# Both halves of a LayerNorm-closed output projection by Strassen-Winograd products, with some sums made by adding DMAs

## The chip, the core and the metric

The kernel runs on one NeuronCore of one Trainium2 chip. The metric is the time of one execution on the device in microseconds, median of three runs. Beside it stands one profiled execution, whose trace gives a start and a duration for every instruction. The engines are PE (matrix products; PEld is its weight load), DVE (vector), ACT (scalar), POOL (GpSimd) and SP, which only issues DMAs.

## The reference, cut to what matters

One step of a hybrid encoder layer for a prompt of 256 tokens and a running stream of 32, 288 rows together, width 1024. A single input projection feeds an mLSTM branch and a sparse attention branch. Both are gated and mixed, and the mix goes through the output projection, a residual and a LayerNorm:

```python
mixed = jax.nn.sigmoid(ga) * (branch_a @ w_out_a) + jax.nn.sigmoid(gb) * (branch_b @ w_out_b)
return layer_norm(DN_ALPHA * x + mixed @ w_o, ln_g, ln_b)
```

Everything is float32. The outputs besides the rows `y` are keys, values, indexer keys and the mLSTM states `C`, `n`, `m`. The change touches `mixed @ w_o` for the 256 prompt rows, the LayerNorm behind it, and the order in which the last outputs are stored.

## The kernel before, in words

**Two halves for every number.** PE multiplies in a rounded format (`F32R`). Each operand is split into a high half (rounded by an ACT copy) and a low half (raw minus high, a DVE subtraction, line 194 or 176). A product is three matmuls: high times high, high times low, low times high (lines 1062 to 1064 for projections, `group`, line 1073, for the output projection).

**Tiles and their order.** `tile_order` (line 60) lists the weight tiles of 128 columns by 1024 rows; each is one stage of 24 matmuls on PE, 3.2 us. The last sixteen are `ga`, `wa` in turn for j = 0 to 7. `WO` is the position of the first of the eight tiles of `w_o`. The main loop (line 1298) issues in each stage t: loads (`load_plan`, line 89), the low half of tile t + 2, the evacuation of tile t - 1, the high half of tile t + 3, then the 24 matmuls, with `side()` in their middle, which runs the jobs that `at(slot, ...)` put there. The order in which instructions are written is the order of every queue; nothing reorders them. Pairs of split tiles (`wh`, `wl`) rotate through four buffers each, raw tiles through eight `wst` buffers.

**Evacuating the mixed rows.** `wa` tile j (line 1005) gives rows 128 j to 128 j + 127 of the transposed mix `mB`, and their halves `mxh`, `mxl`; POOL copies the 32 sample columns to `mxs` (line 1014).

**The output projection** (`finish`, line 1159). The prompt rows form two blocks (rows 1 and 2), the contraction of 1024 is cut in two halves, and the output columns in two. The first half of the contraction (512) is done by Winograd's form of Strassen's scheme with seven block products: sums of token blocks s1 to s4 (`token_sums`, line 1017) and of weight blocks t1 to t4 (`weight_sum`, line 1034, four DVE subtractions). `seventh` (line 1079) is one such product: two contraction blocks of 128, three matmuls of 512 columns each. The second half is done plainly: `plain` (line 1085), four quarters of twelve matmuls. The partial results gather in PSUM banks `y11`, `y12`, `y21`, `y22`; `begun` and `added` (DVE, lines 1163 and 1167) put them onto the residual `z`, reading one bank twice where two outputs share a sum. `sample_rows` (line 1091) does the 32 sample rows in 64 small matmuls from raw tiles.

**The end.** `recorded` and `centred` take the statistics and centre rows, `scaled` multiplies by the reciprocal deviation (made by POOL's power, line 1156) and adds the bias. The first 128 rows are scaled and stored (line 1247) before the second 128 rows are begun. `state_prompt(h)` (line 776) makes the state of head h: twelve matmuls, two ACT copies, and a store, by SP for heads 0 and 1, by ACT for 2 and 3. In program order: first rows' store; second rows' centring; states 0 to 2; second rows' scaling and two stores by halves; state 3.

Of the kernel before, what the change touches and what calls it, by code (L numbers as in the profile page):

```python
# [14 lines left out]
OP = mybir.AluOpType  # L15
# [16 lines left out]
SEVEN = ("b11", "b21", "t2", "t1", "t3")  # L32
# [53 lines left out]
EARLY = WO - 20  # L86


def load_plan():
    slots, homes = defaultdict(list), {}  # L90
    for t in range(FIRST, EARLY + 9):
        slots[max(t - 9, FIRST)].append(t)
        homes[t] = (t - FIRST) % 8
    for i in range(4):
        slots[EARLY + i].append(WO + i)
        homes[WO + i] = (EARLY + 9 + i - FIRST) % 8
    rest = [*range(EARLY + 9, WO), *range(WO + 4, NT)]
    for i, t in enumerate(rest):
        slots[EARLY + 4 + i].append(t)
        homes[t] = (EARLY + 13 + i % 4 - FIRST) % 8  # L100
    return slots, homes
# [10 lines left out]
def body(ctx, tc, a, o):  # L112
# [37 lines left out]
    def load_tile(t):  # L150
        if t >= NT or t in loaded:
            return
        loaded.add(t)
        stage[t] = sb(f"wst{t}", [128, KT * 128], tag=f"wst{HOMES[t]}")
        sp.dma_start(stage[t], a["w"][:, t - FIRST])
# [5 lines left out]
    def raw_unit(u):  # L161
        if u[0] == "t":
            return lazy["sums"][u]
        if u[0] == "b":
            return stage[POS["wo", ("b11", "b12", "b21", "b22").index(u)]]
        return stage[POS["wo", int(u[1])]]
# [7 lines left out]
    def unit_lo(u):  # L174
        wh, wl = split[u]
        dve.tensor_tensor(wl, raw_unit(u), wh.bitcast(F32), OP.subtract)

# [30 lines left out]
    zeros = sb("zeros", [128, 128], BF)  # L208
# [95 lines left out]
    wn = sb("wn", [128, 8])  # L304
    wp0 = sb("wp0", [128, 4])
    ws = sb("ws", [128, 2])
# [628 lines left out]
    def evac(t, p):  # L935
# [69 lines left out]
        elif n == "wa":  # L1005
            if j == 0:
                lazy["mxh"] = sb("mxh", [128, 8, T], F32R, tag="a4")
                lazy["mxl"] = sb("mxl", [128, 8, T], F32R, tag="a2")
                lazy["mxs"] = sb("mxs", [128, 8, TS])
# [5 lines left out]
            halves("mxh", "mxl", j, mx)  # L1015

    def token_sums():
        m = lazy["mB"]
        a11, a12 = m[:, 0:2, 0:128], m[:, 2:4, 0:128]
        a21, a22 = m[:, 0:2, 128:256], m[:, 2:4, 128:256]  # L1020
        s1, s2, s3, s4 = (lazy["sraw"][:, i].rearrange("p (k t) -> p k t", k=2) for i in range(4))
# [5 lines left out]
    def token_halves():  # L1027
        both = sb("sums", [128, 2, 4, 256], F32R, tag="kaT")
        act.copy(both[:, 0], lazy["sraw"])
        dve.tensor_tensor(both[:, 1], lazy["sraw"], both[:, 0].bitcast(F32), OP.subtract)  # L1030
        for i in range(4):
            lazy["s", i + 1] = tuple(both[:, e, i].rearrange("p (k t) -> p k t", k=2) for e in range(2))

    def weight_sum(name):
        if "sums" not in lazy:
            t = sb("t123", [128, 3, KT * 128], tag="a5")
            lazy["sums"] = {"t1": t[:, 0], "t2": t[:, 1], "t3": t[:, 2], "t4": sb("t4", [128, KT * 128], tag="wmat")}
        first, second = {"t1": ("b12", "b11"), "t2": ("b22", "t1"), "t3": ("b22", "b12"), "t4": ("b21", "t2")}[name]
        dve.tensor_tensor(lazy["sums"][name], raw_unit(first), raw_unit(second), OP.subtract)

    at(WO - 6, token_sums)
    at(WO - 4, token_halves)
    for i, n in enumerate(("t1", "t2", "t3", "t4")):
        at(EARLY + 5 + 2 * i, weight_sum, n)
# [22 lines left out]
    def standing(n):  # L1067
        if n[0] == "s":
            return lazy["s", int(n[1])]
        k, r = 2 * (n[2] == "2"), 128 * (n[1] == "2")  # L1070
        return tuple(lazy[m][:, k:k + 2, r:r + 128] for m in ("mxh", "mxl"))
# [7 lines left out]
    def seventh(p, x, u, first=False):  # L1079
        x = standing(x)  # L1080
# [4 lines left out]
    def plain(p, rows, column, first=False):  # L1085
        r = slice(128 * rows, 128 * rows + 128)
        for k in range(4, KT):
            group(p, (lazy["mxh"][:, k, r], lazy["mxl"][:, k, r]), split[f"w{k}"],
                  slice(512 * column, 512 * column + 512), first and k == 4, k == KT - 1)

    def sample_rows(p):
        for k in range(KT):
            for q in range(4):
                if k < 4:
                    w, c = stage[POS["wo", 2 * (k // 2) + q // 2]], 512 * (k % 2) + 256 * (q % 2)
                else:
                    w, c = stage[POS["wo", k]], 256 * q
# [33 lines left out]
    def load_tail():  # L1131
        lazy["xn"] = sb("xn", [128, 2, D], tag="vaT")
        sq = sb("sq", [128, 8, 256], tag="stC")
        lazy["zs"], lazy["gs"], lazy["bs"], lazy["xs"] = (sq[:, i] for i in range(4))
        lazy["sraw"] = sq[:, 4:8]
        lazy["bst"] = sb("bst", [128, 2, 2, 6], tag="sg", bufs=3)
        lazy["bss"] = sb("bss", [128, 4, 6])
        sp.dma_start(lazy["xn"], a["x_nat"][0:TP].rearrange("(b p) c -> p b c", p=128))
        sp.dma_start(lazy["xs"], ap_of(a["x_nat"], TP * D, [[256, 4], [D, TS], [1, 256]]))

    def load_affine():
        gb = sb("rest", [128, 2, D], tag="xhl")
        lazy["g"], lazy["b"] = gb[:, 0], gb[:, 1]
        sp.dma_start(gb, ap_of(a["ln_gb"], 0, [[0, 128], [D, 2], [1, D]]))
# [6 lines left out]
    def statistics(b, r, records):  # L1151
        mv = sb(f"mv{b}", [128, 2])
        nr = sb(f"nr{b}", [128, 2])
# [5 lines left out]
    def finish():  # L1159
        z, zs, bst, bss = lazy["xn"], lazy["zs"], lazy["bst"], lazy["bss"]  # L1160
        g, be = lazy["g"], lazy["b"]

        def begun(b, c, p):
            half = slice(512 * c, 512 * c + 512)
            dve.scalar_tensor_tensor(z[:, b, half], z[:, b, half], ALPHA, p, op0=OP.mult, op1=OP.add)

        def added(b, c, p):
            half = slice(512 * c, 512 * c + 512)
            dve.tensor_tensor(z[:, b, half], z[:, b, half], p, OP.add)

        def recorded(b, c):
            dve.bn_stats(bst[:, b, c], z[:, b, 512 * c:512 * c + 512])

        def centred(b):
            mv, nr = statistics(b, slice(0, 128), bst[:, b].rearrange("p a b -> p (a b)"))
            dve.scalar_tensor_tensor(z[:, b], z[:, b], mv[:, 0:1], g, op0=OP.subtract, op1=OP.mult)
            return nr[:, 1:2]

        def scaled(b, rs):
            for c in (slice(0, 512), slice(512, 1024)):  # L1180
                dve.scalar_tensor_tensor(z[:, b, c], z[:, b, c], rs, be[:, c], op0=OP.mult, op1=OP.add)

        def put(c):
            c = slice(512 * c, 512 * c + 512)
            sp.dma_start(o["y"][128:256, c], z[:, 1, c])

        own = sb("wown", [128, 2, KT * 128], F32R, tag="a1")
        spare = sb("spare", [128, 2, KT * 128], F32R, tag="a3")
        lazy["oc"] = sb("oc_all", [128, AH, 2, CROW], tag="a6")
        pool.memset(lazy["oc"][:, :, :, 257:], 0.0)  # L1190
        y11, y12, y21, y22 = (bank(f"yn{i}") for i in range(4))
        p = bank("yns")

        r = slice(96, 128)
        unit_lo("t2")
        evac(WO - 1, prev)
        seventh(y21, "a11", "b11", True)
        seventh(y11, "a12", "b21", True)
        unit_hi("t1")
        begun(0, 0, y21)  # L1200
        unit_lo("t1")
        sample_rows(p)
        unit_hi("t3")
        unit_lo("t3")
        unit_hi("w4")
        unit_lo("w4")
        unit_hi("w7", (own[:, 0], own[:, 1]))
        unit_lo("w7")
        seventh(y21, "s2", "t2")
        dve.scalar_tensor_tensor(zs, lazy["xs"], ALPHA, p[:, 0:256], op0=OP.mult, op1=OP.add)  # L1210
        dve.bn_stats(bss[:, 3], zs)
        begun(0, 1, y21)
        unit_hi("w5")
        unit_lo("w5")
        seventh(y12, "s1", "t1", True)
        begun(1, 1, y12)
        unit_hi("w6")
        unit_lo("w6")
        seventh(y21, "s3", "t3")
        unit_hi("b22")  # L1220
        unit_lo("b22")
        added(1, 1, y21)
        plain(y11, 0, 0)
        unit_hi("t4", (spare[:, 0], spare[:, 1]))
        unit_lo("t4")
        for q in range(3):
            dve.tensor_copy(bss[r, q], bss[32 * q:32 * q + 32, 3])
        mv, nr = statistics(2, r, bss[r].rearrange("p a b -> p (a b)"))
        for q in range(4):
            pool.tensor_copy(nr[32 * q:32 * q + 32, 0:1], mv[r, 0:1])  # L1230
        for q in range(3):
            pool.tensor_copy(nr[32 * q:32 * q + 32, 1:2], nr[r, 1:2])
        seventh(y12, "s4", "b22")
        plain(y12, 0, 1)
        added(0, 0, y11)
        recorded(0, 0)
        dve.scalar_tensor_tensor(zs, zs, nr[:, 0:1], lazy["gs"], op0=OP.subtract, op1=OP.mult)
        dve.scalar_tensor_tensor(zs, zs, nr[:, 1:2], lazy["bs"], op0=OP.mult, op1=OP.add)
        sp.dma_start(ap_of(o["y"], TP * D, [[256, 4], [D, TS], [1, 256]]), zs)
        seventh(y21, "a22", "t4")  # L1240
        plain(y21, 1, 0)
        plain(y22, 1, 1, True)
        added(0, 1, y12)
        recorded(0, 1)
        rs = centred(0)
        scaled(0, rs)
        sp.dma_start(o["y"][0:128], z[:, 0])
        begun(1, 0, y21)
        recorded(1, 0)
        added(1, 1, y22)  # L1250
        recorded(1, 1)
        rs = centred(1)
        for h in range(AH - 1):
            state_prompt(h)
        scaled(1, rs)
        for c in range(2):
            put(c)
# [14 lines left out]
    for h in range(AH):  # L1272
        at(POS["ga", 4] + h, k_weighted, h)
# [51 lines left out]
def pack_weights(x, w_in, w_out_a, w_out_b, w_o):  # L1325
# [3 lines left out]
    for t, (n, j) in enumerate(ORDER):  # L1329
# [6 lines left out]
        if n == "wo":  # L1336
            if j < 4:
                k, c = 256 * (j // 2), 512 * (j % 2)
# [64 lines left out]
```

## Time and profile before

| what | us |
|---|---|
| median of 3 runs (412.32 to 412.84) | 412.34 |
| the profiled execution | 411.89 |
| its span | 410.2 |
| PE busy in the span | 405.1 |
| DVE busy | 330.3 |
| ACT busy | 220.6 |
| first product of the output projection starts | 375.75 |
| first product of the states starts | 400.48 |
| last store is issued | 407.02 |

The span is the time from the first to the last event of the trace. A row of a timeline reads: start, duration, engine, line, operation, output <- input by the program's names, shapes, count. In brackets stands the time for which the engine was idle before it, and what released it. A row with a count above 1 covers several instructions, one behind the other. The DMA view cuts a window into 40 slices and gives the share of the DMA engines that were busy, in tenths, and the GB/s moved.

### The profile page before, as it was taken

Reading aid. Unit: us, or ns where it says so; the run is one execution under the profiler, and the core shown is the slowest. Engines: PE = TensorE matmul, PEld = TensorE weight load, DVE = VectorE, ACT = ScalarE, POOL = GpSimd, SP = SyncE. Lnnn points to the kernel's source line nnn. Section 1 sums busy time; section 2 is a strip of 40 time slices with the busy share of each in tenths; the row PEclk is TensorE's granted clock in tenths of the full one; section 3 lists DMA queues with packets and bytes.
Section 4 is the critical chain, followed back from the end, with each engine's and each line's share of the span. In section 5 each row is a group of like instructions: output and inputs, shape, how many; then the busy total and the mean of one; then the engine's idle time right before and its main releaser. Section 6 shows DMA issues by size and latency. Waiting matters only on the chain.

```text
span 410.2 us, 8482 instructions
## 1 busy us (share of the span) xinstructions
PE 405.1 (99%) x3111; PEld 394.3 (96%) x3111; DVE 330.3 (81%) x674; ACT 220.6 (54%) x426; POOL 197.2 (48%) x448
## 2 busy tenths in 40 slices
PE   8999999999999999999999999999999999999996
PEld 6999999999999999999989999999999999998785
DVE  5878979997885878887968878988766677788985
ACT  5797563543765665576645545654444335474502
POOL 0210059993388657769800028547799846000031
PEclk9999999999999999999999999999999999999999
DMA  8987979787955655559943674454656557545005
GB/s 294 393 299 164 340 262 322 257 187 232 400 161 155 228 158 162 163 188 195 288 128 120 163 260 118 148 155 123 185 156 200 161 154 257 170 151 176 5 15 211
DMA packets 43151, 81.09 MB, mean 198 GB/s; under 512 B 20682, under 2 KB 25670, under 8 KB 42182
## 3 DMA queue, kind: packets, MB, share of 16 engines
q1 hardware_dynamic: 42390, 79.73, 62.2%
q10 hardware_dynamic: 720, 0.82, 0.6%
q8 instruction: 24, 0.39, 0.4%
q14 instruction: 17, 0.14, 0.1%
HBM read 73.38 MB, written 9.06 MB: 201 GB/s over the span
## 4 chain that ended last, share of the span: by engine, by line
PE 97%; DMA 1%; ACT 0%; SPq 0%; ACTq 0%; issue 0%; DVE 0%
PE pj L1063 27%; PE pj L1064 27%; PE pj L1062 27%; PE yn L1077 5%; PE pj L1126 1%; DMA wst_k<-in_first 1%; PE pj L1121 1%; PE yns L1098 1%; PE pj L1124 0%; PE ix L484 0%; PE al L640 0%; PE s L704 0%; PE av L673 0%; PE c L788 0%; PE c L786 0%; PE os L616 0%
## 5 line engine op out<-in xcount | busy, mean ns | idle before, releaser
L1063 PE MATMUL pj<-xhl,wh 128*128 128x288 f32 x704 | 207.7, 295 | 0.0
L1062 PE MATMUL pj<-xhl,wh 128*128 128x288 f32 x704 | 207.6, 295 | 0.0
L1064 PE MATMUL pj<-xhl,wl 128*128 128x288 f32 x704 | 207.5, 295 | 0.0
L194 DVE TENSOR_TENSOR wl<-wst,wh 128x1024 fp32r<-128x1024 f32 x104 | 129.8, 1249 | 13.8 <-ACT wh L186 13.5
L1062 PEld LDWEIGHTS pj<-xhl,wh 128*128 128x128 f32 x704 | 132.4, 188 | 0.6 <-issue 0.5
L1063 PEld LDWEIGHTS pj<-xhl,wh 128*128 128x128 f32 x704 | 132.4, 188 | 0.0
L1064 PEld LDWEIGHTS pj<-xhl,wl 128*128 128x128 f32 x704 | 132.3, 188 | 0.0
L186 ACT CAST wh<-wst 128x1024 fp32r<-128x1024 f32 x104 | 109.1, 1049 | 10.7 <-PE pj L1063 5.1
L141 POOL COPY pt<-bm 32x96 f32<-32x96 f32 x128 | 48.8, 381 | 19.9 <-DVE bm L656 10.7
L141 POOL COPY kaT<-kn 32x128 f32<-32x128 f32 x64 | 32.8, 513 | 5.1 <-DVE kn L754 2.5
L141 POOL COPY vn<-qaT 32x128 f32<-32x128 f32 x64 | 29.0, 453 | 2.6
L141 POOL COPY hn<-qaT 32x128 f32<-32x128 f32 x32 | 15.5, 485 | 12.1 <-DVE qaT L730 5.6
L141 POOL COPY hn<-ht 32x128 f32<-32x128 f32 x32 | 14.7, 459 | 9.3 <-DVE ht L730 8.0
L1062 PE MATMUL pj<-bah,wh 128*128 128x288 f32 x64 | 18.9, 296 | 0.0
L1063 PE MATMUL pj<-bal,wh 128*128 128x288 f32 x64 | 18.9, 296 | 0.0
L1064 PE MATMUL pj<-bah,wl 128*128 128x288 f32 x64 | 18.9, 296 | 0.0
L1062 PE MATMUL pj<-bbh,wh 128*128 128x288 f32 x64 | 18.9, 295 | 0.0
L1063 PE MATMUL pj<-bbl,wh 128*128 128x288 f32 x64 | 18.9, 295 | 0.0
L1064 PE MATMUL pj<-bbh,wl 128*128 128x288 f32 x64 | 18.8, 294 | 0.0
L999 ACT ACTIVATE sg<-pj 128x288 f32<-128x288 f32 x16 | 6.6, 410 | 22.1 <-PE pj L1064 22.1
L1014 POOL COPY mxs<-mB 128x32 f32<-128x32 f32 x8 | 1.9, 243 | 30.6 <-DVE mB L1013 30.5
L932 ACT CAST mxh<-mB 128x288 fp32r<-128x288 f32 x8 | 3.5, 433 | 22.2 <-DVE mB L1013 22.2
(510 smaller groups left out, 682.9 us busy)
## 6 DMA issues: line engine op xcount, KB each, us to landing
wst<-in_w SPq DMA_DIRECT2D x112, 512.0 KB, 4.1
wst_k<-in_first SPq DMA_DIRECT2D x5, 440.0 KB, 6.7
rscr<-rrow SPq DMA_DIRECT2D x2, 768.0 KB
out_k<-kbT SPq DMA_DIRECT2D x1, 1152.0 KB, 10.0
vrows<-vat SPq DMA_DIRECT2D x8, 144.0 KB, 1.8
stC<-in_state_C SPq DMA_DIRECT2D x1, 1028.0 KB
out_C_sample<-stC SPq DMA_DIRECT2D x1, 1028.0 KB
bm<-rscr SPq DMA_DIRECT2D x1, 1024.0 KB
```

What stands on the lines that cost most here:

```text
L141: pool.tensor_copy(out(quads[k], quads[i]), turned(quads[i], quads[k]))
L186: act.copy(split[t][0], stage[t])
L194: dve.tensor_tensor(wl, stage[t], wh.bitcast(F32), OP.subtract)
L932: act.copy(lazy[hi][:, j], v)
L999: act.activation(sg, q, AF.Sigmoid)
L1062: pe.matmul(p[:, :T], lhsT=wh[:, c], rhs=h[:, k], start=(k == 0), stop=False)
L1063: pe.matmul(p[:, :T], lhsT=wh[:, c], rhs=l[:, k], start=False, stop=False)
L1064: pe.matmul(p[:, :T], lhsT=wl[:, c], rhs=h[:, k], start=False, stop=(k == KT - 1))
L1077: pe.matmul(p, lhsT=l, rhs=r, start=first and i == 0, stop=last and i == 2, skip_group_check=True)
L1098: pe.matmul(p[32 * q:32 * q + 32, 0:256], lhsT=lazy["mxs"][:, k], rhs=w[:, c:c + 256], start=(k == 0), stop=(k == KT - 1))
L1121: pe.matmul(q, lhsT=part, rhs=xh[:, k, new], start=False, stop=(k == KT - 1))
L1126: pe.matmul(p[t][:, 0:2 * n].rearrange("p (a n) -> p a n", a=2), lhsT=part, rhs=xhl[:, :, k, new], start=False, stop=False)
```

## The change

Both halves of the contraction are now done by seven block products each: `b11` to `b22` are the four weight blocks of the first half, `c11` to `c22` of the second, `t1` to `t4` and `u1` to `u4` their sums. All eight `w_o` tiles are packed as blocks. `plain` and the bank `y22` are gone. In `finish` each product of the first half is followed by its twin of the second half into the same bank.

Sums come from two sources. `t1`, `t2`, `t3`, `u1`, `u2` stay DVE subtractions (`difference`). The weight sums `t4`, `u3`, `u4`, and the low halves of the first half's token sums, of a part of the second half's, and of `b22` and `c22`, are made by `less`: ACT writes the negated (for a low half: negated and rounded) tile, and a DMA that POOL issues adds the other tile to it in place. The token sums of the second half are taken in two pieces, the second of them in `finish`, since it needs the last `wa` tile. The high half of `b22` is taken five stages ahead of the output projection.

Loads: the four `b` tiles come five stages earlier, the `c` tiles in two loads of 1 MB, at 14 and 10 stages before `WO`; the first residual rows (`z0`) five stages before it; the second rows (`z1`), the gain and the bias only when the sample rows have used the raw `b` tiles, into whose buffers they go. `k_weighted` moves one stage forward. Small tiles change buffers.

At the end the order on DVE and SP is new: the first rows are centred, then the second rows are begun and centred; the states 0 and 1 are made and stored; then the first rows are scaled and stored; state 2; then the second rows by halves; state 3.

```diff
-EARLY = WO - 20
+EARLY = WO - 25
...
+    def less(out, taken, added):
+        act.mul(out, taken, -1.0)
+        pool.dma_start(out.bitcast(F32), added, accum_op=OP.add)
+
+    def unit_summed(u, home):
+        if u not in split:
+            unit_hi(u, home)
+        less(home[1], raw_unit(u), raw_unit(u))
...
+    def halves_summed(i):
+        less(halves_of(i, 1), lazy["sraw"][i], lazy["sraw"][i])
...
+    def summed(name, taken, added):
+        load_tile(name)
+        less(stage[name], raw_unit(taken), raw_unit(added))
...
+    at(WO - 7, first_sums)
+    at(WO - 2, lambda: token_sums(1, slice(0, 1), lazy["sraw"][1]))
+    at(WO - 5, early_hi)
+    at(WO - 4, summed, "t4", "t2", "b21")
+    at(WO - 3, summed, "u3", "c12", "c22")
+    at(WO - 3, summed, "u4", "u2", "c21")
+    at(WO - 1, halves_hi, 0)
+    for i, n in enumerate(("t1", "t2", "t3")):
+        at(EARLY + 6 + i, difference, n)
+    at(WO - 14, load_two, WO + 4, "vaT")
+    at(WO - 10, load_two, WO + 6, "stC")
+    at(WO - 6, difference, "u1")
+    at(WO - 5, difference, "u2")
```

The new `finish`, after its helpers (lines of the new kernel, in order):

```python
        split_lo(WO + 2)
        unit_hi("c21")
        evac(WO - 1, prev)
        unit_lo("c21")
        halves("mxh", "mxl", KT - 1, lazy["mB"][:, KT - 1])
        halves_summed(0)
        unit_hi("t2")
        halves_hi(1)
        halves_summed(1)
...
        seventh(y21, "a11", "b11", True)
        seventh(y21, "a11", "c11")
        seventh(y11, "a12", "b21", True)
        seventh(y11, "a12", "c21")
        token_sums(1, slice(1, 2), lazy["sraw"][2])
        begun(0, 0, y21)
        unit_lo("t2")
        unit_hi("u2")
        unit_lo("u2")
        halves_hi(2)
        halves_lo(2)
...
        unit_summed("b22", split["b22"])
        added(0, 0, y11)
        unit_hi("t1")
        unit_lo("t1")
        unit_hi("u1")
        unit_lo("u1")
        unit_summed("c22", home("spare", "a3"))
        sample_rows(p)
        for i, n in enumerate(("z1", "g", "b")):
            HOMES[n] = HOMES[WO + i]
            load_tile(n)
...
        seventh(y21, "s2", "t2")
        seventh(y21, "s2", "u2")
        unit_hi("t3")
        begun(0, 1, y21)
        unit_lo("t3")
        seventh(y12, "s1", "t1", True)
        seventh(y12, "s1", "u1")
        unit_hi("u3")
        unit_lo("u3")
        begun(1, 1, y12)
        seventh(y21, "s3", "t3")
        seventh(y21, "s3", "u3")
...
        added(1, 1, y21)
        recorded(1, 1)
        seventh(y12, "s4", "b22")
        seventh(y12, "s4", "c22")
        dve.scalar_tensor_tensor(zs, zs, nr[:, 0:1], lazy["gs"], op0=OP.subtract, op1=OP.mult)
        added(0, 1, y12)
        recorded(0, 1)
        seventh(y21, "a22", "t4")
        seventh(y21, "a22", "u4")
        rs = centred(0)
        dve.scalar_tensor_tensor(zs, zs, nr[:, 1:2], lazy["bs"], op0=OP.mult, op1=OP.add)
        sp.dma_start(ap_of(o["y"], TP * D, [[256, 4], [D, TS], [1, 256]]), zs)
        begun(1, 0, y21)
        recorded(1, 0)
        rs1 = centred(1)
        for h in range(AH - 2):
            state_prompt(h)
        dve.scalar_tensor_tensor(z[0], z[0], rs, be, op0=OP.mult, op1=OP.add)
        sp.dma_start(o["y"][0:128], z[0])
        state_prompt(AH - 2)
        for c in range(2):
            dve.scalar_tensor_tensor(z[1][:, col[c]], z[1][:, col[c]], rs1, be[:, col[c]], op0=OP.mult, op1=OP.add)
            sp.dma_start(o["y"][128:256, col[c]], z[1][:, col[c]])
        state_prompt(AH - 1)
```

More of the change, by code (lines that the diff above doesn't have):

```diff
@@ L1008, in evac @@
                 lazy["mxl"] = sb("mxl", [128, 8, T], F32R, tag="a2")
-                lazy["mxs"] = sb("mxs", [128, 8, TS])
+                lazy["mxs"] = sb("mxs", [128, 8, TS], tag="hns")
             sg = tmp_sig["ga", j]
@@ L1014, in evac, with token_sums @@
             pool.tensor_copy(lazy["mxs"][:, j], mx[:, TP:T])
-            halves("mxh", "mxl", j, mx)
-    def token_sums():
+            if j < KT - 1:
+                halves("mxh", "mxl", j, mx)
+    def token_sums(half, blocks, out):
         m = lazy["mB"]
-        a11, a12 = m[:, 0:2, 0:128], m[:, 2:4, 0:128]
-        a21, a22 = m[:, 0:2, 128:256], m[:, 2:4, 128:256]
-        s1, s2, s3, s4 = (lazy["sraw"][:, i].rearrange("p (k t) -> p k t", k=2) for i in range(4))
+        k = slice(4 * half + blocks.start, 4 * half + blocks.stop)
+        k2 = slice(k.start + 2, k.stop + 2)
+        a11, a12, a21, a22 = m[:, k, 0:128], m[:, k2, 0:128], m[:, k, 128:256], m[:, k2, 128:256]
+        s1, s2, s3, s4 = (out.rearrange("p (i k t) -> p i k t", i=4, t=128)[:, i] for i in range(4))
         dve.tensor_tensor(s1, a21, a22, OP.add)
@@ new lines, in halves_summed, with halves_lo, halves_of, early_hi @@
+    def halves_summed(i):
+        less(halves_of(i, 1), lazy["sraw"][i], lazy["sraw"][i])
+    def halves_lo(i):
+        dve.tensor_tensor(halves_of(i, 1), lazy["sraw"][i], halves_of(i, 0).bitcast(F32), OP.subtract)
+    def halves_of(i, e):
+        v = lazy["halves"][:, int(i > 0), e]
+        return v if i == 0 else v[:, 512 * i - 512:512 * i]
+    def summed(name, taken, added):
+        load_tile(name)
+        less(stage[name], raw_unit(taken), raw_unit(added))
+    def early_hi():
+        extra = sb("extra", [128, KT * 128], F32R)
+        act.copy(extra, raw_unit("b22"))
+        lazy["b22"] = extra
@@ new lines, in difference @@
+    def difference(name):
+        first, second = {"t1": ("b12", "b11"), "t2": ("b22", "t1"), "t3": ("b22", "b12"),
+                         "u1": ("c12", "c11"), "u2": ("c22", "u1")}[name]
+        if name == "t1":
+            t = sb("t123", [128, 3, KT * 128], tag="a5")
+            lazy.update(t1=t[:, 0], t2=t[:, 1], t3=t[:, 2])
+        if name == "u1":
+            t = sb("u12", [128, 2, KT * 128], tag="kaT")
+            lazy.update(u1=t[:, 0], u2=t[:, 1])
+        dve.tensor_tensor(raw_unit(name), raw_unit(first), raw_unit(second), OP.subtract)
@@ L1065, in product, with standing @@
         return p
-    def standing(n):
+    def standing(n, half):
         if n[0] == "s":
-            return lazy["s", int(n[1])]
-        k, r = 2 * (n[2] == "2"), 128 * (n[1] == "2")
-        return tuple(lazy[m][:, k:k + 2, r:r + 128] for m in ("mxh", "mxl"))
+            v = [lazy["halves"][:, half, e] for e in range(2)]
+            order = "p (k i t) -> p i k t" if half else "p (i k t) -> p i k t"
+            return [u.rearrange(order, i=4, k=2)[:, int(n[1]) - 1] for u in v]
+        k, r = 4 * half + 2 * (n[2] == "2"), 128 * (n[1] == "2")
+        return [lazy[m][:, k:k + 2, r:r + 128] for m in ("mxh", "mxl")]
     def group(p, x, w, c, first=False, last=False):
@@ L1083, in seventh @@
             group(p, [v[:, k] for v in x], w, slice(512 * k, 512 * k + 512), first and k == 0, k == 1)
[L1085 to L1089, printed above, removed]
     def sample_rows(p):
@@ L1177, in centred, with home @@
             return nr[:, 1:2]
[L1179 to L1188, printed above, removed]
+        def home(name, tag):
+            v = sb(name, [128, 2, KT * 128], F32R, tag=tag)
+            return v[:, 0], v[:, 1]
@@ L1189, in finish @@
+        y11, y12, y21 = (bank(f"yn{i}") for i in range(3))
+        p = bank("yns")
+        split_lo(WO + 2)
+        unit_hi("c21")
+        evac(WO - 1, prev)
+        unit_lo("c21")
[4 more added lines that the diff above has]
+        halves_summed(1)
         lazy["oc"] = sb("oc_all", [128, AH, 2, CROW], tag="a6")
         pool.memset(lazy["oc"][:, :, :, 257:], 0.0)
-        y11, y12, y21, y22 = (bank(f"yn{i}") for i in range(4))
@@ L1228, in finish @@
[L1228 to L1232, printed above, removed]
+        seventh(y21, "s3", "u3")
+        unit_hi("t4")
+        unit_lo("t4")
+        unit_hi("u4")
+        unit_lo("u4")
+        for i in range(3):
+            act.copy(bss[r, i], bss[32 * i:32 * i + 32, 3])
+        mv, nr = statistics(2, r, bss[r].rearrange("p a b -> p (a b)"))
@@ L1238, in finish @@
+        recorded(0, 1)
+        seventh(y21, "a22", "t4")
+        seventh(y21, "a22", "u4")
+        rs = centred(0)
         dve.scalar_tensor_tensor(zs, zs, nr[:, 1:2], lazy["bs"], op0=OP.mult, op1=OP.add)
         sp.dma_start(ap_of(o["y"], TP * D, [[256, 4], [D, TS], [1, 256]]), zs)
[L1240 to L1247, printed above, removed]
```

165 lines of the change are left out of this document (71 added, 94 removed).

## The prediction, made before the changed kernel was run

> **What bounds the kernel now.** I read the page first, then the busy table by stages for the last 20 projection tiles, then the timelines of PE, DVE, ACT and SP from 372 us on, and last the DMA view in 0.2 us slices for the last 8 us.
>
> ```profile
> span 410.2 us, 8482 instructions
> PE 405.1 (99%) x3111; PEld 394.3 (96%) x3111; DVE 330.3 (81%) x674; ACT 220.6 (54%) x426; POOL 197.2 (48%) x448
> ...
> PE 97%; DMA 1%; ACT 0%; SPq 0%; ACTq 0%; issue 0%; DVE 0%
> ```
> PE is the chain from start to end. The profiled execution took 411.89 us, 1.69 more than its span, and the median of the runs is 412.34, 0.45 above that execution. I work in the trace's own clock and add the difference to the median.
>
> ```profile
> core 0: us, PE busy (x) PEld busy (x) DVE busy (x) ACT busy (x) POOL busy (x), PEclk, DMA share, GB/s
> ...
> sum 63.70, PE 63.70 PEld 63.70 DVE 46.78 ACT 30.19 POOL 27.19; mean PE 3.19 PEld 3.19 DVE 2.34 ACT 1.51 POOL 1.36
> ```
> These are the 20 stages of one tile each, 311.6 to 375.3 us: PE has no gap, DVE and ACT have room. Then comes the output projection:
>
> ```profile
> 375.75 0.40 PE L1077 MATMUL yn<-wh_b,mxh 128*128 128x512 f32 x1
> 378.63 3.66 PE L1098 MATMUL yns<-wst,mxs 128*32 128x256 f32 x64
> 382.23 0.50 PE L1077 MATMUL yn<-wh_t,sums 128*128 128x512 f32 x1
> 400.48 0.28 PE L786 MATMUL c<-v1h,kx 128*128 128x258 f32 x1
> 406.14 0.29 PE L788 MATMUL c<-v1h,kx 128*128 128x258 f32 x1
> ```
> Twelve products, the sample rows, 78 products, then 48 for the states. The 78 take 400.48 - 382.23 = 18.25 us, 0.234 each, without a gap. But PE is not what ends last. Behind it stand the stores:
>
> ```profile
> 399.68 0.34 SPq L1247 DMA_DIRECT2D out_y<-xn  x1
> 402.58 1.72 SPq L793 DMA_DIRECT2D out_C_prompt<-oc_all  x2
> 405.14 0.99 SPq L1185 DMA_DIRECT2D out_y<-xn  x2
> 405.42 0.36 ACTq L793 DMA_DIRECT2D out_C_prompt<-oc_all  x1
> 406.23 0.35 ACTq L791 DMA_DIRECT2D out_C_prompt<-oc_all  x1
> 407.02 0.34 ACTq L791 DMA_DIRECT2D out_C_prompt<-oc_all  x1
> ```
> ```profile
> DMA  0089960009997019999999999999920000000000
> GB/s 0 0 337 413 403 240 0 0 0 370 381 359 272 11 61 328 399 410 341 370 457 377 391 389 369 346 364 354 370 82 0 0 0 0 0 0 0 0 0 0
> ```
> ```profile
> out_C_prompt<-oc_all SPq DMA_DIRECT2D x2, 272.0 KB, 2.1
> ...
> out_y<-xn SPq DMA_DIRECT2D x1, 512.0 KB
> out_y<-xn SPq DMA_DIRECT2D x2, 256.0 KB
> ```
> The slices run from 403.0 in steps of 0.2. A store issued at 405.14 moves data from 405.96 (0.82 later), and from there the DMA engines are full until 408.85: 2.89 us for 1056 KB (256 + 272 + 256 + 136 + 136), 374 GB/s. Then 1.35 us more to the end at 410.2. So the end is a drain: what counts is when it starts and how many bytes are in it. The 512 KB of the first rows are not in it. They left at 399.68:
>
> ```profile
> GB/s 0 0 0 0 0 0 0 0 0 0 0 0 0 0 0 492 410 328 410 369 451 451 328 492 410 369 410 328 0 0 0 0 0 0 0 0 0 0 0 0
> ```
> (slices of 0.1 from 399.0: 1.3 us, 403 GB/s, with the DMA engines idle before and after).
>
> **The change, part by part. Products.** Before: 7 products of blocks times 2 contraction blocks times 3 = 42 matmuls, and 4 plain quarters times 4 times 3 = 48, together 90. After: 14 times 2 times 3 = 84. Six fewer at 0.234: 1.40 us off PE. The sample rows keep 64. If PE never waits, the states' products start at 399.08 instead of 400.48, and all that follows from them moves by 1.40.
>
> **Does PE wait?** Durations, each for one tile:
>
> ```profile
> 378.55 2.36 DVE L176 TENSOR_TENSOR wl_t<-t,wh_t 128x1024 fp32r<-128x1024 f32 x2
> 377.45 1.99 ACT L172 CAST wh_t<-t 128x1024 fp32r<-128x1024 f32 x2
> 376.62 0.46 DVE L1013 TENSOR_TENSOR mB<-sg,mB 128x288 f32<-128x288 f32 x1
> 359.26 0.42 DVE L1022 TENSOR_TENSOR sq<-mB 128x256 f32<-128x256 f32 x1
> 394.34 0.48 DVE L1238 SCALAR_TENSOR_TENSOR sq<-sq,nr 128x256 f32<-128x256 f32 x1 [0.30 <-POOL nr L1232]
> 394.74 0.68 DVE L1169 TENSOR_TENSOR xn<-xn,yn 128x512 f32<-128x512 f32 x1
> 395.46 0.69 DVE L1172 BATCH_NORM_STATS2 bst<-xn 128x6 f32<-128x512 f32 x1
> 396.19 0.21 DVE L1154 BATCH_NORM_AGGREGATE mv<-bst 128x2 f32<-128x12 f32 x1
> 396.50 1.28 DVE L1176 SCALAR_TENSOR_TENSOR xn<-xn,mv,rest 128x1024 f32<-128x1024 f32 x1
> ```
> Low half 1.18, high half 1.00. Ahead of the output projection, DVE gains two weight differences (2.4) and four sums of 128 columns (about 1.0 by the row of 256), and loses one difference and the low half of the sums (2.4). ACT gains three negations, one early copy and one high half, and loses one (some 4 us over six stages where it has 1.7 free in each). Splits stand two tiles ahead of their use, so this hides; uncovered it would cost up to 1 us. The same goes for the other load order: each late tile is asked for at least two stages (6.4 us) before its split, and this row says how long it takes:
>
> ```profile
> wst<-in_w SPq DMA_DIRECT2D x112, 512.0 KB, 4.1
> ```
> On SP the two double loads stand ahead of single ones and `z0` ahead of nothing urgent: hidden. `z1`, `g`, `b` wait for the sample rows to leave their buffers (about 382.7) and land from 387 on; `z1` is needed at 390.8. SP's later stores wait for work after 399 anyway.
>
> Inside the tail I walked the five queues in program order. DVE does ten low halves instead of nine, one of half size, four small sums more, and one addition fewer; the three small copies go to ACT: about 1.5 us more work in 1.4 us less time, where it now sits idle for some 1.9. The products start at 375.75, with 4 times 1.40 before the sample rows, at 385.0 `s2 t2`, then every 1.40 the next, to 399.06. Low halves by the walk against their need: `t3` 389.8 against 390.6, `u3` 391.0 against 392.0, `y21` free at 394.8 against 396.2. All fit, by 0.8 us or more. Cover gone, the excess goes straight onto PE.
>
> **The adding DMAs** have no row. Seven are issued by POOL, each after an ACT negation; behind them on POOL stand only the border memset and the small statistics, needed after 394. `t4`, `u3`, `u4` start some 20 us ahead of need. The tight one is the low half of the first sums: ACT takes `c21` (when the last projection tile frees its pair, 375.95), the last mixed tile (377.3), the negation (to 378.4); its product is due at 385.0. That leaves 6.6 us for issue and landing. Bounds: 2.1 us, the row of a 272 KB store, and 10.0, the longest landing that has a row:
>
> ```profile
> out_k<-kbT SPq DMA_DIRECT2D x1, 1152.0 KB, 10.0
> 396.73 1.47 POOL L1156 TENSOR_TENSOR nr<-mv,mhalf 128x1 f32<-128x1 f32 x1 [2.43 <-DVE mv L1155]
> ```
> For POOL's issue I take 1.0, between nothing and its 1.47 for a tiny operation. For the landing I take 4.1, the load of the same size: it lands at 383.5, 1.5 us early. At the upper bounds PE would wait 378.4 + 1.5 + 10.0 - 385.0 = 4.9 us; at the lower, none. The others have at least 2.5 us of slack by the same prices.
>
> The Trainium skill, "DMA: Bandwidth & Descriptors", section "Anatomy of one DMA", prices a DMA issued by GpSimd at 2.0 us plus bytes over 436 GB/s, an estimate of 3.2 us for 512 KB, for a plain copy; with it nothing waits either, and no run shown so far tests it.
>
> **The stores.** The third state's store would be issued at 405.42 - 1.40 = 404.02, data from 404.84. The first rows are now scaled only after the second rows have been centred. DVE: addition, statistics, aggregate and centring take 394.74 to 397.78 = 3.04 now. After: the first rows' last product group ends near 396.4; 3.04; the sample rows' scaling 0.4; 3.04 for the second rows (their product has ended by then, at 399.3); 1.28 for the scaling: about 404.1. So 512 KB that left at 399.68 now leave at 404.1, with data from 404.9, inside the drain. It then holds 1056 + 512 = 1568 KB. The old 1056 at their 2.89 us, the new 512 at their own 1.3: 4.19 us from 404.84, ending at 409.03 against 408.85 now. The second rows' halves (DVE done by 405.2) and the last state (405.6) come in time to keep it full. Sum: start 1.12 earlier than 405.96, contents 1.30 longer: +0.18. With all bytes at 403 GB/s the drain takes 3.98 us: -0.03; all at 374, 4.29: +0.28. I take the middle, +0.1: a span of 410.3, an execution near 412.0 and a median of 412.4. What PE saves, the stores give back. If the first rows come 0.6 us later still, nothing changes, since the third state's store fills the time.
>
> **Rivals.** First, slower: the first sums' adding DMA lands late. An addition has to read its destination as well as its source; at twice the load's 4.1, plus 1.0, it lands at 387.6 and PE waits 2.6 us, with all else moved: +0.1 + 2.6, about 415.0. The point from which it decides is 6.6 us from negation to landing. For it: nothing else this tight lies on the path. Against: the rows of that size are 4.1 and less.
>
> Second, faster: the end follows the last issue, not the bytes. The chain of waits names PE for 97%, and if the stores ran beside each other without delay, the last state's store would go 1.40 us earlier and so would the end: 410.9. Against it stand the full slices from 405.96 to 408.85; for it, that some slices reach 457 and 492 GB/s, and at 457 the drain would end 0.5 us earlier.
>
> Third, POOL's issue is held up while DVE works. DVE's busy tenths in slices of 10.26 us:
>
> ```profile
> DVE  5878979997885878887968878988766677788985
> ```
> From 369 to 390 they read 8 and 9 (the 37th and 38th). If the issue waited out two low halves (2.36) on top of 1.0, landing would be 385.9 and PE would wait 0.8: 413.2. The Trainium skill, "SBUF — State Buffer", section "SBUF: two separate sides", warns that a DMA issued by GpSimd starves for descriptors while DVE runs in a two-port mode; its section "Who interferes with whom" says that `tensor_tensor` did not cause this. DVE's low halves are of that kind, so by the page this price would be nothing; no run shown so far tells.
>
> **How the numbers follow.** A measurement of this kernel can tell about 0.2% (0.8 us). Forecast 0.46, with its own range 411.9 to 412.9. First rival 0.22, nearly all beyond 0.8 us; second 0.25; third 0.07, on the border. Faster: 0.25. Slower: 0.22 and a part of the third, 0.25. Same: 0.50. The range reaches to 410.9 for the second and to 414.4, most of the way to the first.
>
> **What would show it.** Right: 84 matmuls of 512 columns, the states' first product near 399.1, PE without a gap before it, the first rows' store issued near 404, and full DMA slices from 404.8 to 409. Wrong: a gap of PE ahead of `s2 t2` with a DMA as releaser (first or third rival), or DMA slices with idle time after 405 (second), or the first rows' store issued before 403.

## The result and the profile after

The changed kernel takes 414.73 us (median of 6 runs, 414.54 to 415.35), beside 412.33 for the kernel before in the same series: a ratio of 1.0059, 95% interval 1.0047 to 1.0072, so 2.4 us slower. The forecast was 412.4. Its profiled execution took 414.71, with a span of 413.0.

The page of the changed kernel, its first lines and its chain of waits:

```profile
span 413.0 us, 8517 instructions
...
PE 404.8 (98%) x3105; PEld 393.4 (95%) x3105; DVE 331.5 (80%) x679; ACT 231.1 (56%) x441; POOL 206.5 (50%) x455
...
PE 85%; DVE 6%; ACT 3%; DMA 2%; issue 2%; ACTq 0%; DVEq 0%
```

Six matmuls fewer, as forecast (3111 to 3105), yet the span is 2.8 longer than before. The chain of waits, 97% PE before, now runs back from the end over the states and PE to the landing of one DMA (`spare<-two`, the add for the low half of `c22`), and from its issue back over DVE and ACT, so that PE has only 85% of it. PE's timeline shows where PE stands, with the first product of the output projection and the first of the states:

```profile
375.78 0.39 PE L1138 MATMUL yn<-wh_b,mxh 128*128 128x512 f32 x1
...
385.02 0.50 PE L1138 MATMUL yn<-wh_t,halves 128*128 128x512 f32 x1
...
387.63 0.73 PE L1138 MATMUL yn<-wh_u,halves 128*128 128x512 f32 x2 [0.49 <-DMA halves<-sraw]
395.46 0.50 PE L1138 MATMUL yn<-wown,halves 128*128 128x512 f32 x1 [0.90 <-DMA wown<-wst]
397.30 1.43 PE L1138 MATMUL yn<-spare,halves 128*128 128x512 f32 x5 [0.18 <-DMA spare<-two]
401.34 0.28 PE L807 MATMUL c<-v1h,kx 128*128 128x258 f32 x1
```

PE reaches `s2 t2` at 385.02, where the forecast had 385.0. Then it waits three times, each time for the landing of an adding DMA: for the low half of the second part of the token sums (`s2 u2`), for that of `b22` (`s4 b22`) and for that of `c22` (`s4 c22`). Measured by the starts of neighbouring products, which stand 0.23 apart elsewhere, the three breaks cost 0.66, 1.07 and 0.34 us, and the restart at 395.46 another 0.11: 2.2 us. The states' products, forecast for 399.08, start at 401.34, 2.3 later.

The POOL issues of these DMAs and, from the DMA view, the landings (KB of each, median us from issue to landing):

```profile
379.15 0.89 POOL L193 DMA_DIRECT2D halves<-sraw  x1 [0.58 <-ACT halves L192]
381.14 0.86 POOL L193 DMA_DIRECT2D halves<-sraw  x1 [1.09 <-ACT halves L192]
383.56 0.87 POOL L193 DMA_DIRECT2D wown<-wst  x1 [1.35 <-ACT wown L192]
387.57 0.85 POOL L193 DMA_DIRECT2D spare<-two  x1 [3.15 <-DVE zs L1269]
```
```profile
wstu<-two POOLq DMA_DIRECT2D x2, 512.0 KB, 7.2
wstt<-wst POOLq DMA_DIRECT2D x1, 512.0 KB, 4.7
halves<-sraw POOLq DMA_DIRECT2D x1, 512.0 KB, 4.6
wown<-wst POOLq DMA_DIRECT2D x1, 512.0 KB, 11.9
spare<-two POOLq DMA_DIRECT2D x1, 512.0 KB, 9.7
halves<-sraw POOLq DMA_DIRECT2D x1, 256.0 KB, 6.5
```

The same add of 512 KB takes 4.6 us for the first sums and 11.9 for `b22`. From issue to the moment at which PE stood ready there were 6.0 us (387.14 - 381.14), 11.0 (394.56 - 383.56) and 9.5 (397.12 - 387.57); the landings took 6.5, 11.9 and 9.7, which are late by the idle times that PE's rows show. Where the time goes is in the table by stages (busy time of each engine, granted clock, DMA share, GB/s):

```profile
core 0: us, PE busy (x) PEld busy (x) DVE busy (x) ACT busy (x) POOL busy (x), PEclk, DMA share, GB/s
380.50:383.30 2.80, 2.80 (x41) 1.67 (x43) 2.60 (x3) 2.80 (x5) 1.07 (x2) 1.00 1.00 187
383.30:387.60 4.30, 3.84 (x44) 2.21 (x34) 4.26 (x7) 4.30 (x5) 0.89 (x2) 1.00 0.98 237
387.60:395.40 7.80, 6.93 (x29) 5.37 (x29) 6.74 (x10) 4.07 (x7) 0.91 (x2) 1.00 0.98 232
395.40:398.00 2.60, 2.36 (x9) 1.65 (x10) 1.67 (x3) 0.00 (x0) 1.87 (x8) 1.00 0.14 27
```

The DMA engines read as full from 380.5 to 395.4 (shares of 0.98 to 1.00), at half to six tenths of the 374 to 403 GB/s that full engines moved in the stores before. In the first row adds run alone: 187 GB/s, 2.8 us for 512 KB. And there are plain loads in between, issued by SP in the same microseconds:

```profile
382.53 0.33 SPq L159 DMA_DIRECT2D wstz<-in_x_nat  x1
382.90 0.44 SPq L161 DMA_DIRECT2D wstg<-in_ln_gb  x1
383.53 0.59 SPq L161 DMA_DIRECT2D wstb<-in_ln_gb  x1
```

The DMA view names the queues. `q0` is POOL's, with 3.41 MB in the whole execution, the bytes of the seven adding DMAs; `q1` is SP's. A row gives packets, MB and the share of the 16 engines' time. From 380.5 to 395.4:

```profile
q0 software_dynamic: 543, 1.77, 63.3%
q1 hardware_dynamic: 432, 1.57, 34.4%
```

Of the 14.9 us the adds hold the engines for 9.4 (63.3%) and the three loads, 1536 KB, for 5.1 (34.4%). Hardly anything is left over, and the two don't share evenly. From 387.0 to 389.5 the view reads:

```profile
q1 hardware_dynamic: 107, 0.42, 70.1%
q0 software_dynamic: 1, 0.00, 0.0%
```

The add for `b22` was issued at 383.56, but in these 2.5 us POOL's queue moves nothing, while the loads keep the engines 70% busy. The first packet of that add starts at 389.87, 6.3 us after its issue. The residual rows, gain and bias came in front of `b22`'s and `c22`'s adds.

The end of the changed kernel. SP's and ACT's last issues, and the drain in slices of 0.2 us from 406:

```profile
403.43 1.71 SPq L814 DMA_DIRECT2D out_C_prompt<-oc_all  x2
406.39 0.33 SPq L1312 DMA_DIRECT2D out_y<-wstz  x1
407.05 1.66 SPq L1316 DMA_DIRECT2D out_y<-wstz  x2
...
407.94 0.83 ACTq L812 DMA_DIRECT2D out_C_prompt<-oc_all  x1
```
```profile
DMA  9930018999989999999999999982000000000000
GB/s 381 370 120 22 41 54 337 458 408 420 419 335 394 409 389 380 370 370 340 406 348 389 381 374 329 366 271 82 0 0 0 0 0 0 0 0 0 0 0 0
```

The first rows' store now goes at 406.39, 2.3 after the forecast's 404.1, as all the rest. The engines are full from 407.2 to 411.45, 4.3 us, where the forecast had 4.19 (bounds 3.98 and 4.29).

### The profile page after: what moved, and what is told of

It reads as the page before. It is cut to its first block, busy times and chain, and to the rows that moved or that the text cites. A ratio compares the mean times of both kernels' runs of the same rounds, so it can differ in the third digit from the quotient of the medians.

```text
span 413.0 us, 8517 instructions
## 1 busy us (share of the span) xinstructions
PE 404.8 (98%) x3105; PEld 393.4 (95%) x3105; DVE 331.5 (80%) x679; ACT 231.1 (56%) x441; POOL 206.5 (50%) x455
## 3 DMA queue, kind: packets, MB, share of 16 engines
q0 software_dynamic: 1008, 3.41, 4.4%
## 4 chain that ended last, share of the span: by engine, by line
PE 85%; DVE 6%; ACT 3%; DMA 2%; issue 2%; ACTq 0%; DVEq 0%
PE pj L1122 24%; PE pj L1123 24%; PE pj L1121 24%; DMA spare<-two 2%; PE pj L1178 1%; DVE wl L216 1%; PE yn L1138 1%; ACT wh L208 1%; PE pj L1173 1%; DVE mB L1034 1%; DVE kx L794 1%; PE pj L1171 1%; DVE wl_b L189 1%; DVE sg L1033 1%; PE ix L505 0%
## 5 line engine op out<-in xcount | busy, mean ns | idle before, releaser
L142 POOL COPY kaT<-kn 32x128 f32<-32x128 f32 x64 | 34.2, 535 | 4.1 <-DVE kn L775 1.4
L142 POOL COPY hn<-qaT 32x128 f32<-32x128 f32 x32 | 16.6, 519 | 12.0 <-DVE qaT L751 5.5
L142 POOL COPY hn<-ht 32x128 f32<-32x128 f32 x32 | 15.7, 491 | 9.2 <-DVE ht L751 7.9
L1035 POOL COPY mxs<-mB 128x32 f32<-128x32 f32 x8 | 3.0, 375 | 27.6 <-DVE mB L1034 27.6
```

The costliest lines, as they stand in the source:

```text
L142: pool.tensor_copy(out(quads[k], quads[i]), turned(quads[i], quads[k]))
```

## The experiments

The theory after the first trace: an adding DMA holds the DMA engines about twice as long as a plain one; three plain loads stand in the same stretch; so the adds land late and PE waits 2.2 us. The rest of the change is worth nothing, since what PE saves the stores give back. The rivals: a slow issue on POOL, and a second cost somewhere in the change, such as the new end or DVE's and ACT's new work. Traces of different runs stand up to 1.2 us apart at the output projection (375.28 to 376.50), so times of steps below are counted from its first product. Each kernel's ratio is to the kernel before in the same series.

**No adds.** The negations on ACT stay, the DMAs go, so the kernel leaves out seven additions.

```diff
         act.mul(out, taken, -1.0)
-        pool.dma_start(out.bitcast(F32), added, accum_op=OP.add)
```

> The adding DMAs are left out; ACT's negations stay, so three weight sums and the low halves that they make are wrong. Theory (PE waits only for late adding DMAs, and the end is a drain of the stores that now holds the first rows): no wait of PE, states' first product near 399.1, and still no gain: 412.4 us against 412.3 before. Rival (the end follows PE, the stores run beside it): 410.9.

Measured: 412.60 us (10 runs; before 412.13), ratio 1.0017, 1.0008 to 1.0026. PE waits nowhere. The states start 23.18 us after the first product, 1.55 earlier than before (24.73). The kernel is nevertheless slower than before, by 0.5 us in the medians and 0.3 to 1.1 by the interval. So 1.7 of the 2.4 us (by the ratios, 0.0042 of 412) belong to the adds, and a PE that is 1.55 us earlier brings nothing at the end, as the forecast had it. The three loads, now without adds beside them, still hold the engines for 5.2 us (`q1` at 65.0% of the 8 us from 382), where their bytes at 390 GB/s, the middle of the 374 to 403 that the stores reached, would take 4.0.

**Plain copies in place of adds**, the same bytes from the same queue at the same times.

```diff
-        pool.dma_start(out.bitcast(F32), added, accum_op=OP.add)
+        pool.dma_start(out.bitcast(F32), added)
```

> Each adding DMA becomes a plain copy of the same tile by POOL (the sums are wrong). Theory (an addition holds the DMA engines twice as long as a copy): the copies land 2.5 to 6 us after their issue, PE waits nowhere, 412.4 us. Rival (any DMA that POOL issues is this slow): landings of 6 to 12 us as now, 414.7.

Measured: 412.26 (10 runs), ratio 1.0006, 0.9996 to 1.0016. No wait of PE. The landings:

```profile
wstu<-two POOLq DMA_DIRECT2D x2, 512.0 KB, 5.5
wstt<-wst POOLq DMA_DIRECT2D x1, 512.0 KB, 3.1
halves<-sraw POOLq DMA_DIRECT2D x1, 512.0 KB, 2.9
wown<-wst POOLq DMA_DIRECT2D x1, 512.0 KB, 8.6
spare<-two POOLq DMA_DIRECT2D x1, 512.0 KB, 7.0
halves<-sraw POOLq DMA_DIRECT2D x1, 256.0 KB, 2.2
```

With adds, `wstt` and the 512 KB of `halves` took 4.7 and 4.6, `wown` 11.9, `spare` 9.7 and the 256 KB 6.5. So adding costs landing time that the same bytes don't, and POOL's issue is a small part of it (0.54 us here, 0.85 to 0.89 there). The 8.6 for `wown` and the 7.0 for `spare`, both above the 6 that the theory allowed, show the other half. Beside the three loads a copy too takes nearly three times as long as alone: from 384.1, when it is issued, to 389.2 the view lists packets of `q1` alone.

The Trainium skill, "DMA: Bandwidth & Descriptors", section "Anatomy of one DMA", gives 2.0 us plus bytes over 436 GB/s, an estimate of 3.2 for 512 KB. The copy alone agrees with 2.9 and 3.1; the add at 4.6 and 4.7 doesn't, and for it the measurement decides.

**Gain and bias out of the way.** They are loaded into the buffers of `u3` and `t4`, when those have been used.

```diff
-        for i, n in enumerate(("z1", "g", "b")):
-            HOMES[n] = HOMES[WO + i]
-            load_tile(n)
+        HOMES["z1"] = HOMES[WO]
+        load_tile("z1")
...
         unit_lo("u3")
+        HOMES["g"] = HOMES["u3"]
+        load_tile("g")
...
         unit_lo("t4")
+        HOMES["b"] = HOMES["t4"]
+        load_tile("b")
```

> Gain and bias (1 MB) go into the buffers of u3 and t4 and so load some 9 us later. Theory (the two late adding DMAs share full DMA engines with the loads of second rows, gain and bias): 1 MB is 2.7 us of engine time, so b22's landing moves from 395.5 to about 392.8 and c22's to about 394.6, both ahead of need; the wait of 0.7 for the second half's sums stays. 413.3 us. Rival (POOL's DMAs wait for one another, whatever else runs): landings unchanged, 414.7.

Measured: 412.95 (10 runs), ratio 1.0022, 1.0012 to 1.0032. `wown` lands in 6.4 and `spare` in 4.8 us, and of the three waits one is left, that for the add of 256 KB ahead of the loads:

```profile
386.98 0.74 PE L1138 MATMUL yn<-wh_u,halves 128*128 128x512 f32 x2 [0.34 <-DMA halves<-sraw]
```

So two plain loads, moved by some microseconds, take away two of the three waits and 1.5 of the 2.4 us (by the ratios, 0.0037 of 412). Counted from the first product, `b22` lands 5.5 and `c22` 4.9 us earlier than in the changed kernel, where 2.7 was expected from the loads' bytes. That the loads hold up the adds is shown. By what rule POOL's queue stands still behind them is not.

**`b22`'s low half by DVE**, one add less, all else as changed.

```diff
-        unit_summed("b22", split["b22"])
+        unit_lo("b22")
```

> The changed kernel with the low half of b22 taken by DVE (1.14 us more there) instead of an adding DMA. Theory (engine time): 512 KB of additions, 2.8 us, leave the window from 382 to 395; c22 lands some 6 us after its issue, the wait for b22 and c22 is gone, that for the second half's sums stays at 0.3 to 0.7. 413.0. Rival (POOL's DMAs are slow by themselves): c22 still lands 9 to 10 us after its issue, 414.

Measured: 413.15 (8 runs; before 411.96), ratio 1.0027, 1.0014 to 1.0039. No wait of PE at all, though one was expected to stay; `spare` lands in 6.5, the 256 KB in 6.0. One subtraction of DVE's in place of one add removes all three waits.

**The old kernel with the new order of the end**: in `before`, the first rows are scaled and stored only behind the states 0 and 1 and their second centring.

```diff
-        scaled(0, rs)
-        sp.dma_start(o["y"][0:128], z[:, 0])
...
-        rs = centred(1)
-        for h in range(AH - 1):
+        rs1 = centred(1)
+        for h in range(AH - 2):
             state_prompt(h)
+        scaled(0, rs)
+        sp.dma_start(o["y"][0:128], z[:, 0])
+        state_prompt(AH - 2)
```

> The kernel before with the new order of its end alone: first rows scaled and stored after the second rows' centring and the states 0 and 1. PE's work is untouched. Theory (drain): 512 KB enter the drain, which then starts at about 405.6 and takes 4.2 us instead of 2.9 from 406.0: 1.0 us more, 413.1. Rival (the last issue sets the end; it stays at 407.0): no change, 412.1.

Measured: 413.09 (5 runs), ratio 1.0031, 1.0018 to 1.0045: 1.1 us slower than before, for a store whose data nothing in the kernel reads. Its drain is one unbroken stretch (slices of 0.25 us from 403):

```profile
DMA  0000299500899269999999999999999200000000
GB/s 0 0 0 0 87 418 409 200 0 0 313 348 374 79 246 393 393 393 393 366 409 392 390 385 377 341 383 399 393 335 366 70 0 0 0 0 0 0 0 0
```

Full from 406.6 to 410.75, 4.1 us, where 512 KB less took 2.89. The forecast's claim that the end is a drain, priced by its bytes, holds in a kernel that has nothing else of the change.

**The first rows' store in front again.** In the changed kernel, and in the variants without adds and with gain and bias late, the scaling and the store go ahead of the second rows' addition.

```diff
+        dve.scalar_tensor_tensor(z[0], z[0], rs, be, op0=OP.mult, op1=OP.add)
+        sp.dma_start(o["y"][0:128], z[0])
         begun(1, 0, y21)
...
-        dve.scalar_tensor_tensor(z[0], z[0], rs, be, op0=OP.mult, op1=OP.add)
-        sp.dma_start(o["y"][0:128], z[0])
```

> The first rows are scaled and stored before the second rows are begun, as in the kernel before; all else as changed. Theory (the end is a drain): 512 KB leave the drain, DVE's last scaling comes 1.2 us later and then sets the end: 1.0 us less, 413.7. Rival (the last issue sets the end): DVE's last scaling moves it, 1.2 us more, 415.9.

Measured: 414.18 (4 runs; before 412.13), ratio 1.0055, 1.0037 to 1.0074: not to be told from the changed kernel, so the expected 1.0 us less did not come. PE's late states push the two stores together: first rows at 403.32, states 0 and 1 at 403.79, and then one long full stretch again.

> Adding DMAs left out (three weight sums and some low halves are wrong) and the first rows stored early: the most that a cure of both costs could give. Theory: PE's 1.4 us come through once the first rows are out of the drain; DVE's last scaling then ends 0.6 us later than without the early store, and stores of 2.1 MB that start 3 us earlier end about 0.9 us ahead of before: 411.2. Rival (the early store gives nothing, since DVE's queue is full): 412.6 as without adding DMAs.

Measured: 412.68 (10 runs, 411.70 to 413.09; before 412.16), ratio 1.0007, 0.9998 to 1.0017: a miss. Neither PE nor an add stands in the way here, the store is issued at 401.07, and yet 411.2 does not come out.

> Gain and bias loaded late and the first rows stored early; all outputs complete. In late_h1 and late_h1_early DVE stood 1.4 us for an ACT copy, since the low half was put too early in its queue; here that low half stays an adding DMA. Theory: one wait of PE (0.5) is left, the drain starts 3 us earlier with 2.1 MB: 0.5 us ahead of before, 411.6. Rival (DVE's full queue sets the end): 413.0.

Measured: 412.58 (12 runs), ratio 1.0013, 1.0003 to 1.0024; a miss too, with one wait of PE of 0.22 us left. By the ratios, these three and the one in the pair below come out 0.2 to 0.5 us under their twins with the late store, each by less than the intervals resolve.

**The second sums' low half by DVE.** With gain and bias late, the last wait was for the add of 256 KB, so DVE takes it over, first at the place of the add:

```diff
-        halves_summed(1)
+        halves_lo(1)
```

> The changed kernel with gain and bias loaded late, and the low half of the second half's first sums taken by DVE instead of an adding DMA. All outputs are complete. Theory: no wait of PE is left, the states start 1.4 us earlier than before, and the drain takes it back: 412.4. Rival (something else than these DMAs still holds PE): as with the late loads alone, 413.0.

Measured: 413.83 (4 runs; before 411.96), ratio 1.0045, 1.0031 to 1.0059: a clear miss. DVE's timeline and PE's show why:

```profile
380.23 0.69 DVE L1065 TENSOR_TENSOR halves<-sraw,halves 128x512 fp32r<-128x512 f32 x1 [1.40 <-ACT halves L1059]
```
```profile
391.35 0.50 PE L1138 MATMUL yn<-wl_t,halves 128*128 128x512 f32 x1 [0.37 <-DVE wl_t L189]
```

At that place in DVE's queue the instruction waits 1.40 us for ACT's high half, with four token sums and all later low halves behind it. DVE, with 0.8 us to spare by the forecast's walk, has become what is late: its last operation ends 31.0 us after the first product, against 30.2 with gain and bias late alone, and the first rows' store leaves at 29.7 against 28.9. PE's states start 23.8 us after the first product in both.

> As late_h1, and the first rows are scaled and stored before the second rows are begun. Theory: no wait of PE and a drain without the first rows: 1.2 us less than late_h1, 411.3, ahead of both kernels. Rival (DVE's last scaling, 1.2 us later, sets the end): 413.6.

Measured: 413.27 (6 runs), ratio 1.0032, 1.0020 to 1.0043; the same cause.

Then the same three edits with `halves_lo(1)` a few instructions later, behind `t2`'s low half, where ACT has long been done:

```diff
         halves_hi(1)
-        halves_summed(1)
...
         unit_lo("t2")
+        halves_lo(1)
```

> As gb_late_early, with the low half of the second half's first sums on DVE, now behind the low half of t2, where its input is ready. Theory: no wait of PE, DVE 0.6 us more: 411.6, and 1.5 us less than late_h1_early. Rival (DVE's 1.4 us wait was not what late_h1 lost): 413.2 as late_h1_early.

Measured: 411.64 (12 runs, 410.91 to 412.37; before 412.16), ratio 0.9989, 0.9980 to 0.9998. It beats both kernels: 0.5 us under the one before, with an interval that ends just below 1, and 2.9 under the changed one by the ratios. From the kernel just above it differs only in the place of one instruction, which is worth 1.8 us by the ratios. PE waits nowhere. Its stages, set against the same stretch of the changed kernel above, and its stores:

```profile
383.10:387.40 4.30, 4.30 (x47) 2.95 (x39) 4.30 (x6) 4.01 (x5) 1.13 (x2) 1.00 0.97 231
387.40:395.20 7.80, 7.80 (x35) 6.38 (x35) 7.63 (x12) 3.90 (x7) 1.05 (x3) 1.00 0.74 199
```
```profile
401.06 0.35 SPq L1312 DMA_DIRECT2D out_y<-wstz  x1
401.53 1.49 SPq L814 DMA_DIRECT2D out_C_prompt<-oc_all  x2
405.22 0.99 SPq L1321 DMA_DIRECT2D out_y<-wstz  x2
```

PE is busy for 4.30 of 4.30 and 7.80 of 7.80 us, and the DMA share falls from 0.98 to 0.74 where `b22` and `c22` land (5.9 and 4.8 us).

## Why the prediction was wrong

**The step that failed**: "The others have at least 2.5 us of slack by the same prices." The price, 1.0 for the issue and 4.1 for the landing, was near enough for an add that is alone: the first sums took 4.95 us from the end of the negation (378.80) to the landing (383.75), against 5.1. For the others it was not a price at all, since it left out who else holds the engines. Three of them took 6.5, 11.9 and 9.7 us from issue to landing.

Two things were missing. An add holds the engines about twice as long as a copy (187 GB/s at full share). And `z1`, `g`, `b`, which the forecast counted as hidden because nobody needs them early, are themselves in the way. A sum of engine time would have shown it: 9.4 us of adds and 5.1 of loads in 14.9. At the 390 GB/s of plain transfers the same 3328 KB would need only 8.7.

For the 256 KB the sentence did not hold even by its own prices. From the end of its negation (380.79) to the moment at which PE stood ready (387.14) there are 6.35 us, and 1.0 and 4.1 leave 1.25 of them, unless half the bytes are given a shorter landing.

**The right rival at the wrong place.** The first rival named the mechanism, an adding DMA that lands late at twice the load's time, and its size (2.6 us, 415.0), but put it at the first sums. That add came when the engines were free and landed at 383.75 (379.15 + 4.6), 1.3 us before its product. At that place 4.95 us were needed, and the forecast's limit of 6.6 was not reached. One product further 6.35 us were there from negation to need, and the add took 6.84: missed by 0.5.

**Products.** Right: 84 matmuls, and with the adds gone the states start 1.55 us earlier (forecast 1.40).

**DVE and ACT.** Right: no product waits for a split, in the changed kernel or in the one without adds. How thin the 0.8 us were, the experiment with one misplaced instruction shows.

**The stores.** Right in mechanism: the drain of the changed kernel holds the first rows and is full for 4.3 us, and the old kernel with the new order pays 1.1 us for the same bytes. The size is right for the full slices. Take as their end the last moment at which eight of the sixteen engines are busy: counted from the first product it comes at 33.3 us without adds (408.76) and at 33.1 in the kernel before (408.86), +0.2 where the forecast worked out +0.18 and took +0.1. The times are +0.47 without adds and +0.13 with copies; what comes on top stands under what stays open. With PE's waits, 412.4 + 2.2 is 414.6, against 414.73.

**The second rival** (the end follows the last issue) falls with the drain of 4.3 us full, and with the run without adds. There PE's states start 1.55 us earlier and the last store is issued 29.7 us after the first product (405.20) instead of 31.3, and the end does not follow.

**The third** falls too. POOL's issues took 0.85 to 0.89 us beside a DVE that was busy 2.60 of 2.80 us, began 0.35 to 0.6 us after the end of the negation (378.80 to 379.15 for the first sums, 386.98 to 387.57 for `c22`), and were not held up. The row of `c22`'s issue names a DVE instruction as its releaser, but the 0.59 us are 0.58 or 0.59 in every variant with this add, whichever instruction DVE runs there. The sentence of the Trainium skill that the forecast weighed, that `tensor_tensor` doesn't starve such DMAs ("SBUF — State Buffer", "Who interferes with whom"), agrees with these rows.

**What stays open.** Why the kernel without adds and with the early store takes 412.68 while the one with six adds takes 411.64, with the same issue times: first rows 25.52 and 25.47 us after the first product, last state 29.71 and 29.72. The full slices end at 408.0 in both traces, 0.7 us earlier than in the kernel before by the same count. But behind them a remainder of 14 GB/s runs on to 408.9 in the first, and to 408.1 in the second (slices of 0.15 us from 405, first and second kernel):

```profile
GB/s 348 406 450 341 385 319 181 327 402 379 355 348 341 342 362 379 336 396 382 232 55 14 14 14 0 14 0 0 0 0 0 0 0 0 0 0 0 0 0 0
```
```profile
GB/s 392 363 414 377 356 341 181 348 380 390 369 386 328 324 343 388 362 382 410 219 14 0 0 0 0 0 0 0 0 0 0 0 0 0 0 0 0 0 0 0
```

The two profiled executions differ by 0.7 us (412.06 and 411.34), which is this remainder. It is the rest of SP's last stores, and the first trace has one thing in the window that the second has not, a packet of 8 KB of the kind "instruction" at 407.92:

```profile
q14 instruction: 1, 0.01, 0.3%
```

In the profiled execution of every variant with a remainder of 0.7 us or more, from the end of the full slices to the last packet (without adds, and the early store in the changed kernel, without adds and with gain and bias late), such a packet begins within 3 us of that end. In the kernel before and in the fastest one none does. The early store did shorten the full stretch in these three, by 0.9 to 1.1 us against the twin, near the 1.0 first expected of it; a remainder longer by 0.2 to 1.0 us took some or all of that back. Whether the packet makes the remainder, and what decides when it comes, no run here tells; there is one trace of each kernel.

## What to carry to other kernels

A DMA that nobody needs early is not free when another one is on the path: add up all bytes in the stretch, at the rate that each kind reaches, before a landing is priced by a transfer that was alone. Moving work from DVE to an adding DMA trades a busy engine for a shared one. Here one add less took away all three of PE's waits, and two plain loads some microseconds later took away two. And when a kernel ends in a drain of stores, time saved ahead of them brought nothing as long as the first rows' store stayed late; of the five kernels with an early store one came out ahead.

## What the runs showed of the hardware

An add of 512 KB from SBUF to SBUF took 4.6 to 4.7 us from issue to landing, the copy 2.9 to 3.1, each with hardly anything else on the engines; two adds issued 0.9 us apart took 7.2 (median), two copies 5.5. The engines read as full at 187 GB/s under adds. In the packets of the traces, 4 KB of the first sums hold an engine for 0.34 us when they are added and for 0.16 when they are copied (medians). Why an add takes longer was not tried.

A DMA that POOL had issued stood still behind loads of SP's: nothing of `b22`'s add moved for 6.3 us after its issue, in the last 2.5 of them with the engines only 70% busy, and nothing of its copy for 5.2. The first sums' add began to move 1.4 us after its issue.

POOL's copy of the 32 sample columns, 0.21 us in the first six tiles and 0.59 in the seventh, took 1.14 in the last beside a two-input operation of DVE, and ended with it (POOL and DVE of the changed kernel):

```profile
377.43 1.14 POOL L1035 COPY mxs<-mB 128x32 f32<-128x32 f32 x1 [3.88 <-DVE mB L1034]
```
```profile
377.28 1.22 DVE L189 TENSOR_TENSOR wl_c<-two,wh_c 128x1024 fp32r<-128x1024 f32 x1
```

The Trainium skill, "SBUF — State Buffer", section "Who interferes with whom", says that a DVE operation with two SBUF inputs blocks a GpSimd operation that reads SBUF; the two rows agree. Here it cost nothing: POOL's next work, the first add, waited for ACT's negation until 378.80 anyway.
